# Gate products of w_down queued on VectorE behind the step they are written in; the samples' rows of w_down loaded in the other order

## The chip, the cores and the metric

The kernel runs on one core of one Trainium2 chip. The metric is the device time of one execution in microseconds (us), the median of several. A core has five engines, each with an instruction queue of its own that is worked off in order: PE (TensorE, matrix products; PEld is its weight load), DVE (VectorE), ACT (ScalarE), POOL (GpSimd) and SP (SyncE, which here only issues DMAs). Times in rows of the trace count from the first instruction of the profiled execution.

## The reference

One layer of a hybrid recurrent decoder: a token mixer with three head groups, then a gated feed-forward part, for a prompt of 2048 tokens and 8 sample sequences of 4 tokens, all in fp32. The change lies in the feed-forward part:

```python
h = _rmsnorm(x, p['norm_ffn'][l]) * (1 + sc2) + sh2
gate, b_ffn = _causal_dwconv(h @ p['ffn_w_gate'][l], b_ffn, p['ffn_conv_w'][l])
gate = gate + p['ffn_conv_b'][l]
x = x + g2 * ((jax.nn.silu(gate) * (h @ p['ffn_w_up'][l])) @ p['ffn_w_down'][l])
```

The model width is 1024 and the feed-forward width 2816. `g2` is a vector of 1024 numbers per sequence, so for the prompt it can be multiplied into the columns of `ffn_w_down` ahead of the product.

## The kernel before

The program is written in Python as a sequence of steps. A scheduler then orders the instructions of each engine by a simulation of its own: an instruction may be queued ahead of others that are written earlier, where its data allow it and the simulated engine is free. So the place where an instruction is written does not fix its place in its engine's queue. The function that adds an edge "not ahead of this instruction, on the same engine, without a semaphore" is `issue_after`.

Every fp32 product is made of three passes: an operand is split into a rounded part (`w_hi`, a cast on ACT, L1815) and a rest (`w_lo`, a subtraction on DVE, L1816), and PE multiplies hi by hi (L1824), hi by lo and lo by hi (L1825, L1826).

The second half of the prompt goes through a Strassen scheme. In its up stage (`ffn_up_s`), the weights of gate and up come as sets of four 512-column pieces (`w_raw`, 9 buffers). POOL forms sums of these pieces (L1797 to L1803, `s_combo`), ACT and DVE split them into one of four buffers of `w_hi` and `w_lo`, and PE runs seven products a set, each for two groups of tokens, 12 matmuls a product and group, into banks `s_x`, `s_y`, `s_v`. Behind a product (`after`), ACT takes a copy of a bank (`sn`, L1985), DVE adds banks and copies (`add`, L2031) or multiplies up by gate (`mul`, L2032), and the convolution and the activation run on DVE (L1999, L2011, L665), ACT and POOL. PE may write on into a bank only when these readers are done. The sequence has 32 plain products and 140 Strassen products.

Beside this, `down_sums` prepares the weights of the later down stage. It has 11 rows. For each it loads four pieces of `ffn_w_down` (`t_raw`, 8 buffers, so two rows), multiplies each by the gate `g` on DVE (L2176: the gate products, 44 in all), forms four differences on POOL (L2183, 44) and stores the eight results into `wdT` in DRAM (88 stores on SP). The program writes one piece of a row behind each step, from step 40 on, so that 11 rows are written over some 99 of the 172 steps. Nothing of the up stage reads these results: the down stage (`ffn_down_s`) loads them again, from `wdT` into `t_raw`.

In the down stage, `samples` multiplies the 32 sample tokens by the 22 row blocks of the plain `ffn_w_down`: two loads of 128 by 512 for each (`h` 0 and 1, the two halves of the columns), then four small matmuls (L2240, `mm_ds`) that read the half 0, 0, 1, 1.

Of the kernel before, what the change touches and what calls it, by code (L numbers as in the profile page):

```python
# [14 lines left out]
ALU = mybir.AluOpType  # L15
# [59 lines left out]
class Kern:  # L75
# [1840 lines left out]
    def ffn_up_s(self, pts, open1, down):  # L1916

        nc = self.nc
# [64 lines left out]
        def snap(c, ps):  # L1983
            t = self.pev.tile([128, NP], F32, name="sn", tag="sn", bufs=SSN)
            nc.scalar.copy(t, ps)  # L1985
            return t
# [3 lines left out]
        def conv(f, g, U):  # L1990

            n, ns = GS[g][1:]
            y = self.pev.tile([128, NW2], F32, name="sy", tag="ey", bufs=SEY)
            N = n + ns
            cw = self.fcw
            nc.gpsimd.tensor_copy(U[:, 0:2], self.fhalo[:, f, :])
            nc.scalar.activation(y, U[:, 2:], AF.Identity, scale=cw[:, 2, f:f + 1], bias=self.fcb[:, f:f + 1])
            for k in (1, 0):
                nc.vector.scalar_tensor_tensor(y[:, :n], U[:, k:k + n], cw[:, k, f:f + 1], y[:, :n],  # L1999
                                               op0=ALU.mult, op1=ALU.add)  # L2000
            if g == 0:
                nc.gpsimd.tensor_copy(self.fhalo[:, f, :], U[:, n:n + 2])
            else:
                nc.gpsimd.tensor_copy(self.ftails[:, f, 0:2], U[:, n:n + 2])
            if ns:
                us = self.pev.tile([128, NSEQ, NTOK + 2], F32, name="cv_s", tag="cv_s", bufs=2)
                nc.gpsimd.tensor_copy(us[:, :, 0:2], self.sffn[:, f, :].rearrange("p (s k) -> p s k", k=2))
                nc.gpsimd.tensor_copy(us[:, :, 2:], U[:, 2 + n:2 + N].rearrange("p (s t) -> p s t", t=NTOK))
                ys = y[:, n:N].rearrange("p (s t) -> p s t", t=NTOK)
                for k in (1, 0):  # L2010
                    nc.vector.scalar_tensor_tensor(ys, us[:, :, k:k + NTOK], cw[:, k, f:f + 1], ys,  # L2011
                                                   op0=ALU.mult, op1=ALU.add)
                nc.gpsimd.tensor_copy(self.ftails[:, f, 2:18].rearrange("p (s k) -> p s k", k=2), us[:, :, NTOK:])
            hold[f, g] = y

            def act():
                self.silu(y, U[:, 2:], y)
            self.later(1, act)

        def put(f, g, y):  # L2020
            t0 = GS[g][0]
            self.st(self.dram["aT"][f * 128:(f + 1) * 128, t0:t0 + NW2], y)

        def gate_u():
            return self.pev.tile([128, 2 + NW2], F32, name="su", tag="cu", bufs=4)

        def after(s, g, P):
            kind, j, _ = sets[s]
            c = ctx[s, g]
            f1, f2 = 2 * j, 2 * j + 1  # L2030
            add = lambda o, a, b: nc.vector.tensor_tensor(o, a, b, op=ALU.add)  # L2031
            mul = lambda o, b: nc.vector.tensor_tensor(o, o, b, op=ALU.mult)  # L2032
            if P[0] == "C":
                f, h = (f1, f2)[int(P[1]) - 1], (lo_, hi_)[int(P[2]) - 1]
                ps = c[PLAIN_BANK[P]]
                if kind == "u":
                    mul(hold[f, g][:, h], ps)
                    if P[2] == "2":
                        put(f, g, hold.pop((f, g)))
                    return  # L2040
                if P[2] == "1":
                    c[f] = gate_u()
                nc.scalar.copy(c[f][:, 2 + h.start:2 + h.stop], ps)
                if P[2] == "2":
                    conv(f, g, c[f])
                return
            if P in "12":
                if P == "1":
                    c["s1"] = snap(c, c["X"])
                c["n"] = c.get("n", 0) + 1  # L2050
                if c["n"] < 2:
                    return
                s1 = c["s1"]
                if kind == "g":
                    c["U1"] = gate_u()
                    add(c["U1"][:, 2:2 + NP], c["Y"], s1)
                else:
                    add(s1, c["Y"], s1)
                    mul(hold[f1, g][:, lo_], s1)
            elif P == "5":  # L2060
                c["s5"] = snap(c, c["V"])
            elif P == "6":
                c["s2"] = snap(c, c["X"])
            elif P == "3":
                if kind == "g":
                    add(c["U1"][:, 2 + NP:], c["V"], c["s2"])
                    conv(f1, g, c["U1"])
                else:
                    add(c["s2"], c["V"], c["s2"])
                    mul(hold[f1, g][:, hi_], c["s2"])  # L2070
                    put(f1, g, hold.pop((f1, g)))
            elif P == "7":
                if kind == "g":
                    c["U2"] = gate_u()
                    add(c["U2"][:, 2 + NP:], c["X"], c["s5"])
                else:
                    add(c["s5"], c["X"], c["s5"])
                    mul(hold[f2, g][:, hi_], c["s5"])
            elif P == "4":
                if kind == "g":  # L2080
                    nc.scalar.copy(c["U2"][:, 2:2 + NP], c["X"])
                    conv(f2, g, c["U2"])
                else:
                    mul(hold[f2, g][:, lo_], c["X"])
                    put(f2, g, hold.pop((f2, g)))
# [67 lines left out]
    def down_sums(self):  # L2153


        nc = self.nc
        w = self.i["ffn_w_down"][0].rearrange("(k p) c -> p k c", p=128)
        g = self.pev.tile([128, D], F32, name="g2", tag="g2", bufs=1)
        self.ld(g, self.ap(self.dram["modr"], 5 * D, [[0, 128], [1, D]]))
        row = 0  # L2160
        for n, kh in enumerate(KH):
            k0 = 2 * sum(KH[:n])
            for k in range(kh):
                q = {}
                for x in ("11", "12", "22", "21"):
                    i, j = int(x[0]) - 1, int(x[1]) - 1
                    q[x] = r = self.w_raw()[:, :512]
                    self.ld(r, w[:, k0 + kh * i + k, 512 * j:512 * j + 512])

                def put(P, x):  # L2170
                    self.st(self.dram["wdT"]["123B567".index(P) if P != "4" else 7, row], q[x])
                for _ in range(2):
                    yield
                for x, P in (("11", "1"), ("12", "B"), ("22", "3"), ("21", "2")):
                    j = int(x[1]) - 1
                    nc.vector.tensor_tensor(q[x], q[x], g[:, 512 * j:512 * j + 512], op=ALU.mult)  # L2176
                    put(P, x)
                    if x in ("12", "21"):
                        yield
                yield  # L2180
                for P, o, a, b in (("5", "11", "12", "11"), ("7", "12", "22", "12"), ("6", "22", "22", "11"),
                                   ("4", "21", "21", "22")):
                    nc.gpsimd.tensor_tensor(q[o], q[a], q[b], op=ALU.subtract)  # L2183
                    yield
                    put(P, o)
                row += 1
# [37 lines left out]
    def ffn_down_s(self, p, pts, work, freed):  # L2224


        nc = self.nc
# [8 lines left out]
        def sample(k, raw):  # L2236

            done.append(k)
            for j in range(4):
                nc.tensor.matmul(pss[32 * j:32 * j + 32, :256], sam[:, k, :],  # L2240
                                 raw[j // 2][:, 256 * (j % 2):256 * (j % 2) + 256],
                                 start=(len(done) == 1), stop=(len(done) == NFB), tile_position=(0, 32 * j))

        def samples():
            w = self.i["ffn_w_down"][0].rearrange("(k p) c -> p k c", p=128)
            r = []
            for k in range(NFB + 1):
                if k < NFB:
                    r.append([self.w_raw()[:, :512] for _ in range(2)])
                    for h in range(2):  # L2250
                        self.ld(r[k][h], w[:, k, 512 * h:512 * h + 512])
                    yield
                if k:
                    sample(k - 1, r[k - 1])
# [129 lines left out]
        for m, (s, P, U, t, b, begins, ends) in enumerate(seq):  # L2384
            n, q = sets[s]
# [348 lines left out]
```

## Time and profile before

| what | value |
|---|---|
| runs | 2830.92, 2831.51, 2834.84 us, median 2831.51 |
| the profiled execution's own time | 2829.4 us |
| its span, first to last instruction | 2827.7 us |
| mean granted TensorE clock | 0.984 |
| the Strassen up stage on PE (`s_x`, first to last matmul) | 1833.5 to 2339.7 us |
| first and last start of a gate product (L2176) | 1888.2 and 2046.9 us |
| sample products (`mm_ds`) on PE | 2358.2 to 2537.2 us |

A page has a row for each engine with the busy time and the share of the span, and then the span in 40 slices, a digit each: the busy share in tenths, for PEclk the granted clock in tenths of full speed. A row of groups names line, engine, operation and tiles, then the count, the busy time, the mean length of one in ns, and the idle time of the engine ahead of them with what ended it. A row of windows gives, for a stretch, its length and for each engine the busy time with the instruction count behind it, then granted clock, DMA share and GB/s. PE is 96% busy over the whole span, so a time that PE loses in one stretch is not hidden by anything else.

### The profile page before, as it was taken

The numbers are of one execution on the slowest core, as the hardware profiler recorded it, in microseconds if no ns is written. First come the engines' busy times: TensorE is split into PE (matmuls) and PEld (weight loads), VectorE is DVE, ScalarE is ACT, GpSimd is POOL, SyncE is SP. The second block draws the span as 40 slices with busy tenths as digits, with TensorE's granted clock in tenths as the row PEclk, the third lists the DMA queues.
The fourth block names the chain that finished last, engine by engine and source line by source line (L and its number), as shares of the span: only waits on it lengthen the run. The fifth ranks groups of instructions, "written<-read, shape, count | busy, mean of one in ns | idle before, by whom it ended". The sixth has DMA issues, their size and how long they took to land.

```text
span 2827.7 us, 54627 instructions
## 1 busy us (share of the span) xinstructions
PE 2709.6 (96%) x19969; PEld 2461.6 (87%) x19969; DVE 1848.7 (65%) x3785; ACT 1235.5 (44%) x2732; POOL 804.9 (28%) x1272
## 2 busy tenths in 40 slices
PE   6999999999999999999999999988899999999998
PEld 4999888889889999999999989978799996678786
DVE  4535677576666778665565546599976775465765
ACT  4544545455554545544434323443344452232433
POOL 3311223211112422121211101258853441213232
PEclk8999999999999999999999999999999999999999
DMA  6465436575646697554543444687732239786652
GB/s 235 139 203 153 127 111 176 179 228 137 183 151 207 211 288 197 164 150 129 174 143 108 118 144 145 194 255 265 266 120 84 86 91 308 220 285 195 220 167 97
DMA packets 566867, 498.58 MB, mean 176 GB/s; under 512 B 85942, under 2 KB 477782, under 8 KB 565574
## 3 DMA queue, kind: packets, MB, share of 16 engines
q1 hardware_dynamic: 566598, 495.09, 56.8%
q8 instruction: 157, 2.57, 0.4%
q14 instruction: 112, 0.92, 0.1%
HBM read 330.36 MB, written 164.60 MB: 175 GB/s over the span
## 4 chain that ended last, share of the span: by engine, by line
PE 73%; DMA 10%; DVE 8%; issue 3%; ACT 3%; POOL 2%; SPq 1%; DVEq 0%; POOLq 0%; ACTq 0%
PE mm_f L610 10%; PE mm_f L612 10%; PE mm_f L611 10%; PE d_ps L1824 5%; PE d_ps L1826 5%; PE d_ps L1825 5%; PE s_x L1824 2%; PE s_x L1825 2%; PE s_x L1826 2%; PE mm_t L653 2%; PE mm_t L654 1%; PE mm_t L656 1%; DMA w_raw<-oT 1%; DVE w_lo L1816 1%; PE ssq L729 1%
## 5 line engine op out<-in xcount | busy, mean ns | idle before, releaser
L610 PE MATMUL mm_f<-g_hi,w_hi 128*128 128x384 f32 (+2 forms) x2016 | 662.4, 329 | 4.5 <-ACT g_hi L581 4.5
L611 PE MATMUL mm_f<-g_lo,w_hi 128*128 128x384 f32 (+2 forms) x2016 | 652.4, 324 | 0.4 <-DVE g_lo L582 0.4
L612 PE MATMUL mm_f<-g_hi,w_lo 128*128 128x384 f32 (+2 forms) x2016 | 652.0, 323 | 0.0
L610 PEld LDWEIGHTS mm_f<-g_hi,w_hi 128*128 128x128 f32 x2016 | 381.5, 189 | 25.9 <-issue 14.6
L611 PEld LDWEIGHTS mm_f<-g_lo,w_hi 128*128 128x128 f32 x2016 | 382.2, 190 | 6.7 <-issue 4.8
L612 PEld LDWEIGHTS mm_f<-g_hi,w_lo 128*128 128x128 f32 x2016 | 381.8, 189 | 6.4 <-issue 5.7
L1824 PE MATMUL d_ps<-t_hi,w_hi 128*128 128x512 f32 x627 | 250.0, 400 | 5.6 <-ACT w_hi L1815 3.6
L1825 PE MATMUL d_ps<-t_lo,w_hi 128*128 128x512 f32 x627 | 247.3, 395 | 0.0
L1826 PE MATMUL d_ps<-t_hi,w_lo 128*128 128x512 f32 x627 | 243.5, 398 | 0.6 <-DVE w_lo L1816 0.6
L1824 PE MATMUL s_x<-t_hi,w_hi 128*128 128x264 f32 x704 | 204.1, 290 | 20.1 <-ACT sn L1985 8.6
L1826 PE MATMUL s_x<-t_hi,w_lo 128*128 128x264 f32 x704 | 201.7, 288 | 11.3 <-DVE w_lo L1816 11.2
L558 DVE TENSOR_TENSOR w_lo<-w_raw,w_hi 128x512 fp32r<-128x512 f32 (+1 forms) x236 | 163.9, 701 | 73.8 <-ACT w_hi L557 70.3
L1815 ACT CAST w_hi<-a_raw 128x512 fp32r<-128x512 f32 (+1 forms) x159 | 92.8, 584 | 266.2 <-PE d_ps L1825 200.2
L557 ACT CAST w_hi<-w_raw 128x512 fp32r<-128x512 f32 (+1 forms) x236 | 144.2, 619 | 138.6 <-PE mm_f L611 97.0
L1825 PE MATMUL s_x<-t_lo,w_hi 128*128 128x264 f32 x704 | 202.2, 287 | 0.0
L2334 DVE TENSOR_TENSOR d_y<-d_ps,d_y 128x512 f32<-128x512 f32 x159 | 108.8, 687 | 139.0 <-PE d_ps L1826 134.0
L1816 DVE TENSOR_TENSOR w_lo<-w_raw,w_hi 128x512 fp32r<-128x512 f32 x156 | 126.5, 813 | 56.0 <-ACT w_hi L1815 55.3
L1815 ACT CAST w_hi<-w_raw 128x512 fp32r<-128x512 f32 x156 | 96.3, 619 | 147.4 <-PE s_x L1825 50.4
L1824 PEld LDWEIGHTS d_ps<-t_hi,w_hi 128*128 128x128 f32 x627 | 118.1, 188 | 45.3 <-ACT w_hi L1815 11.0
L1824 PEld LDWEIGHTS s_x<-t_hi,w_hi 128*128 128x128 f32 x704 | 134.5, 191 | 23.5 <-ACT sn L1985 9.8
L683 DVE SCALAR_TENSOR_TENSOR qy<-cv_u,par,qy 128x384 f32<-128x384 f32 (+1 forms) x216 | 122.8, 571 | 38.9 <-POOL cv_u L674 23.5
L1826 PEld LDWEIGHTS d_ps<-t_hi,w_lo 128*128 128x128 f32 x627 | 118.1, 188 | 31.6 <-DVE d_y L2334 2.9
(572 smaller groups left out, 6671.3 us busy)
## 6 DMA issues: line engine op xcount, KB each, us to landing
w_raw<-in_w_in_dram SPq DMA_DIRECT2D x96, 256.0 KB
d_y<-x SPq DMA_DIRECT2D x96, 256.0 KB
w_raw<-in_ffn_w_gate_dram SPq DMA_DIRECT2D x94, 256.0 KB
w_raw<-in_ffn_w_up_dram SPq DMA_DIRECT2D x94, 256.0 KB
t_raw<-in_ffn_w_down_dram SPq DMA_DIRECT2D x88, 256.0 KB
wdT<-t_raw SPq DMA_DIRECT2D x88, 256.0 KB
t_raw<-wdT SPq DMA_DIRECT2D x88, 256.0 KB
ada_w<-in_w_ada_dram SPq DMA_DIRECT2D x32, 512.0 KB
```

The lines of the kernel that those rows point to most:

```text
L557: nc.scalar.copy(hi[:, :n], raw[:, :n])
L558: nc.vector.tensor_sub(lo[:, :n], raw[:, :n], hi[:, :n].bitcast(F32))
L610: nc.tensor.matmul(ps[:, :N], wh, hi[:, k, :N], start=(k == 0), stop=False)
L611: nc.tensor.matmul(ps[:, :N], wh, lo[:, k, :N], start=False, stop=False)
L612: nc.tensor.matmul(ps[:, :N], wl, hi[:, k, :N], start=False, stop=(k == 7))
L683: nc.vector.scalar_tensor_tensor(y[:, :n], u[:, j:j + n], cw[:, j, blk:blk + 1], y[:, :n], op0=ALU.mult, op1=ALU.add)
L1815: self.nc.scalar.copy(hi, src)
L1816: self.nc.vector.tensor_sub(lo, src, hi.bitcast(F32))
L1824: self.nc.tensor.matmul(ps, hi[:, k], th, start=(start and k == 0), **f)
L1825: self.nc.tensor.matmul(ps, hi[:, k], tl, start=False, **f)
L1826: self.nc.tensor.matmul(ps, lo[:, k], th, start=False, stop=(k == n - 1), skip_group_check=True)
L2334: add = lambda name, ps: nc.vector.tensor_tensor(xs[s, name], ps, xs[s, name], op=ALU.add)
```

## The change

Two edits. The first remembers the last `add` or `mul` of the up stage that was written (`self.pace`) and writes each gate product inside `issue_after`, so that DVE has it no earlier than behind that instruction. The second swaps the order in which the two halves of a samples' row are loaded. The number of instructions on every engine, their shapes and their data stay the same.

```diff
-            add = lambda o, a, b: nc.vector.tensor_tensor(o, a, b, op=ALU.add)
-            mul = lambda o, b: nc.vector.tensor_tensor(o, o, b, op=ALU.mult)
+            def add(o, a, b):
+                self.pace = nc.vector.tensor_tensor(o, a, b, op=ALU.add)
+
+            def mul(o, b):
+                self.pace = nc.vector.tensor_tensor(o, o, b, op=ALU.mult)
...
                 for x, P in (("11", "1"), ("12", "B"), ("22", "3"), ("21", "2")):
                     j = int(x[1]) - 1
-                    nc.vector.tensor_tensor(q[x], q[x], g[:, 512 * j:512 * j + 512], op=ALU.mult)
+                    with self.tc.issue_after(self.pace.ins):
+                        nc.vector.tensor_tensor(q[x], q[x], g[:, 512 * j:512 * j + 512], op=ALU.mult)
                     put(P, x)
...
-                    for h in range(2):
+                    for h in (1, 0):
                         self.ld(r[k][h], w[:, k, 512 * h:512 * h + 512])
```

Three places show what the scheduler makes of it. A row is a line of the program, the operation, the tiles written and read, the shape, and a count where equal instructions follow each other. The gate product's line is L2176 before and L2180 now; L2031, L2032 and L2183 become L2032, L2035 and L2187.

DVE's queue where the last plain sets end and the first gate product stood, before:

```order
L1811 TENSOR_TENSOR t_raw<-t_raw 128x528
L2176 TENSOR_TENSOR t_raw<-t_raw,g_23409 128x512
L1816 TENSOR_TENSOR w_lo<-w_raw,w_hi 128x512
L1816 TENSOR_TENSOR t_lo<-t_raw,t_hi 128x528 x2
L2032 TENSOR_TENSOR sy<-sy,s_y 128x264 x2
L2176 TENSOR_TENSOR t_raw<-t_raw,g_23409 128x512
L1816 TENSOR_TENSOR w_lo<-w_raw,w_hi 128x512
L665 SCALAR_TENSOR_TENSOR sy<-su,sy 128x528
L1816 TENSOR_TENSOR t_lo<-t_raw,t_hi 128x528
L2176 TENSOR_TENSOR t_raw<-t_raw,g_23409 128x512 x2
L1816 TENSOR_TENSOR t_lo<-t_raw,t_hi 128x528
```

The same place now:

```order
L1811 TENSOR_TENSOR t_raw<-t_raw 128x528
L1816 TENSOR_TENSOR w_lo<-w_raw,w_hi 128x512
L1816 TENSOR_TENSOR t_lo<-t_raw,t_hi 128x528 x2
L2035 TENSOR_TENSOR sy<-sy,s_y 128x264 x2
L1816 TENSOR_TENSOR w_lo<-w_raw,w_hi 128x512
L665 SCALAR_TENSOR_TENSOR sy<-su,sy 128x528
L1816 TENSOR_TENSOR t_lo<-t_raw,t_hi 128x528 x2
```

The gate products are gone from here. Counted over DVE's whole queue by the splits of weights (rows `w_lo<-w_raw`, one for each piece of weights that PE is fed, 156 in the up stage), the first gate product stands behind the 30th split where it stood behind the 17th, and the last behind the 120th where it stood behind the 59th: 44 products over 90 splits in place of 42.

DVE's queue now at the second of the eleven rows of `w_down`, where its four products stand together:

```order
L2011 SCALAR_TENSOR_TENSOR sy<-cv_s,par_970,sy 128x32
L2032 TENSOR_TENSOR su<-s_x,sn 128x264
L2180 TENSOR_TENSOR t_raw<-t_raw,g_23409 128x512 x4
L665 SCALAR_TENSOR_TENSOR sy<-su,sy 128x528
L1999 SCALAR_TENSOR_TENSOR sy<-su,par_970,sy 128x496
L2011 SCALAR_TENSOR_TENSOR sy<-cv_s,par_970,sy 128x32
L1816 TENSOR_TENSOR w_lo<-w_raw,w_hi 128x512
```

They stand behind an add that frees a bank, and ahead of the next split of a weight. Of the eleven rows, six have their four products split into two pairs at two places, and the other five have them in a lump of four like this one.

POOL's queue, where the differences of `down_sums` stand among the sums of weights (L1797 to L1803), in the third Strassen set before:

```order
L1799 TENSOR_TENSOR w_raw<-w_raw 128x512
L2007 COPY cv_s<-sffn 128x8x2
L1801 TENSOR_TENSOR w_raw<-w_raw 128x512
L2183 TENSOR_TENSOR t_raw<-t_raw 128x512 x6
L2007 COPY cv_s<-sffn 128x8x2
L2183 TENSOR_TENSOR t_raw<-t_raw 128x512 x2
L1797 TENSOR_TENSOR w_raw<-w_raw 128x512
```

And the first differences now:

```order
L1797 TENSOR_TENSOR w_raw<-w_raw 128x512
L2187 TENSOR_TENSOR t_raw<-t_raw 128x512
L1803 TENSOR_TENSOR w_raw<-w_raw 128x512
L2187 TENSOR_TENSOR t_raw<-t_raw 128x512 x2
L1799 TENSOR_TENSOR w_raw<-w_raw 128x512
L2187 TENSOR_TENSOR t_raw<-t_raw 128x512
L1801 TENSOR_TENSOR w_raw<-w_raw 128x512
```

Eight differences stood in a row ahead of a sum; now one or two stand between sums here, and at most four anywhere. SP's stores into `wdT` and the loads of `ffn_w_down` move along: the last store stands 12 loads of weights, three sets, ahead of the end of the up stage's 96 loads, where it stood 46 loads ahead.

## The prediction, made before the changed kernel ran

> **What bounds the kernel now.** I read the page first, for the engine that is busy and the slices in which it isn't.
>
> ```profile
> span 2827.7 us, 54627 instructions
> PE 2709.6 (96%) x19969; PEld 2461.6 (87%) x19969; DVE 1848.7 (65%) x3785; ACT 1235.5 (44%) x2732; POOL 804.9 (28%) x1272
> ...
> PE   6999999999999999999999999988899999999998
> ...
> DVE  4535677576666778665565546599976775465765
> ...
> POOL 3311223211112422121211101258853441213232
> ```
>
> PE is busy for 96% of the span. Only the first slice, the last, and slices 27 to 29 (70.7 us each, from 1838 us) fall below nine tenths, and in these three DVE and POOL stand at their highest. So I asked for windows around them, with the bounds at the first gate product and the end of the last.
>
> ```profile
> 1860.00:1888.00 28.00, 21.40 (x163) 20.13 (x163) 27.78 (x35) 15.60 (x29) 19.62 (x18) 1.00 0.63 195
> 1888.00:2048.00 160.00, 131.04 (x981) 127.33 (x982) 157.55 (x196) 53.65 (x109) 130.73 (x106) 0.94 0.79 264
> 2048.00:2100.00 52.00, 50.50 (x414) 50.07 (x413) 39.22 (x66) 21.66 (x43) 28.50 (x31) 1.00 0.50 159
> 2100.00:2300.00 200.00, 200.00 (x1649) 200.00 (x1649) 140.09 (x247) 91.25 (x177) 86.02 (x111) 1.00 0.25 75
> 2358.00:2540.00 182.00, 178.24 (x805) 121.71 (x804) 96.61 (x158) 50.22 (x93) 35.82 (x32) 1.00 0.83 273
> ```
>
> The columns behind the length are busy time and count of PE, PEld, DVE, ACT and POOL, then the granted clock, the DMA share and GB/s. From 2100 to 2300 us the same matmuls run with nothing in the way: 1649 / 200 = 8.245 a microsecond. Against that pace 1888 to 2048 holds 981 / 8.245 = 119.0 us of work in 160 us, a **loss of 41.0 us**. (PE's idle time there, 29.0 us, says less, as the granted clock is 0.94.) From 2048 to 2100 it is 52 - 414 / 8.245 = 1.8 us, and from 1860 to 1888, ahead of all gate products, 28 - 163 / 8.245 = 8.2 us. DVE is busy for 98.5% of the 160 us and for 70% of the undisturbed stretch. The waits of PE from 1888 to 2060 us say who ended them:
>
> ```profile
> PE s_x L1826 <- DVE w_lo L1816: 10.5, 3, 5.3
> PE s_x L1824 <- ACT sn L1985: 8.6, 6, 3.5
> PE s_x L1824 <- DVE sy L2032: 4.7, 1, 4.7
> PE s_x L1824 <- DVE sn L2031: 4.3, 4, 1.6
> ```
>
> DVE ends most of them. ACT was held up in its turn by POOL, as the timeline around 1995 us shows:
>
> ```profile
> 1999.41 0.62 ACT L1815 CAST w_hi<-w_raw 128x512 fp32r<-128x512 f32 x1 [7.00 <-POOL w_raw L1797]
> ...
> 1994.72 2.97 POOL L2183 TENSOR_TENSOR t_raw<-t_raw 128x512 f32<-128x512 f32 x2
> 1997.65 1.73 POOL L1797 TENSOR_TENSOR w_raw<-w_raw 128x512 f32<-128x512 f32 x1
> ```
>
> Two differences of `down_sums` stood ahead of the sum that ACT needed, and ACT idled for 7.00 us with the copies of banks queued behind.
>
> **What the gate products cost where they stand.** The groups of DVE and POOL from 1888 to 2048 us (first five rows), and of DVE from 2100 to 2300 (last three):
>
> ```profile
> L2176 DVE TENSOR_TENSOR t_raw<-t_raw,g 128x512 f32<-128x512 f32 x44 | 44.7, 1026 | 0.5 <-DMA t_raw<-in_ffn_w_down_dram 0.5
> L1816 DVE TENSOR_TENSOR w_lo<-w_raw,w_hi 128x512 fp32r<-128x512 f32 x42 | 42.0, 1008 | 0.1
> L2032 DVE TENSOR_TENSOR sy<-sy,sn 128x264 f32<-128x264 f32 x14 | 13.4, 972 | 0.0
> L1816 DVE TENSOR_TENSOR t_lo<-t_raw,t_hi 128x528 fp32r<-128x528 f32 x4 | 4.9, 1236 | 0.0
> L2183 POOL TENSOR_TENSOR t_raw<-t_raw 128x512 f32<-128x512 f32 x41 | 65.4, 1596 | 11.9 <-DVE t_raw L2176 4.4 <-DVE su L2031 2.6 <-DMA wdT<-t_raw 2.3
> ...
> L1816 DVE TENSOR_TENSOR w_lo<-w_raw,w_hi 128x512 fp32r<-128x512 f32 x69 | 50.8, 736 | 37.6 <-ACT w_hi L1815 37.0
> L2032 DVE TENSOR_TENSOR sy<-sy,sn 128x264 f32<-128x264 f32 x30 | 17.6, 588 | 0.7
> L665 DVE SCALAR_TENSOR_TENSOR sy<-su,sy 128x528 f32<-128x528 f32 x20 | 14.0, 699 | 1.0 <-ACT su L664 1.0
> ```
>
> All 44 gate products fall into the 160 us. They take 44.7 us themselves, and everything else on DVE that reads two tiles is longer while POOL works: the split of a weight 1008 ns against 736, the product into `sy` 972 against 588. In sum, DVE's load that goes with PE's progress is 0.70 x 119.0 = 83.4 us, and 5.6 us belong to the last splits of tokens (`t_lo` 4.9, and one sum of 0.7). What is left of 157.55 is 68.6 us, or **1.56 us for a gate product with its difference on POOL**. So DVE was asked for 157.6 us of work in the 119.0 us that PE needed: it was the bound there, and PE followed it.
>
> **The change, part by part.** The first edit spreads the same 44 products, with their 44 differences on POOL and 88 stores on SP, over 90 splits of weights in place of 42. A split comes every 200 / 69 = 2.90 us at PE's full pace, so that is 261 us, from some 13 splits (38 us) later than 1888 on. DVE's load in them is 0.70 x 261 = 182.8, plus 68.6, together 251.4 us or **96% of 261**. In the 160 us DVE kept itself 98.5% busy, so its floor is 251.4 / 0.985 = 255 us, just under what PE needs. PE becomes the bound again, and of the loss of 41.0 + 1.8 = 42.8 us only what the two engines cost each other at so small a margin stays.
>
> That rest is not in the trace of before as such. Its lower end is 0, as from 2100 to 2300 us. For the upper end I take the two windows with the fewest gate products among others, ten in 40 us:
>
> ```profile
> 1940.00:1960.00 20.00, 18.39 (x151) 18.18 (x150) 20.00 (x27) 5.87 (x12) 17.41 (x11) 1.00 0.85 280
> 1960.00:1980.00 20.00, 18.41 (x148) 17.78 (x146) 18.72 (x26) 7.70 (x13) 16.68 (x21) 1.00 0.82 265
> ```
>
> They hold 299 / 8.245 = 36.3 us of work in 40, a loss of 10%, which would be 26 us over 261. Their density is 0.25 products a microsecond, the changed kernel's 44 / 261 = 0.17. A loss that grows in proportion would give 17 us, one that grows with the square 11 to 12. I take 11, as waiting grows faster than load, and keep 0 and 26.
>
> Every instruction of a moved row was looked at. On SP, 88 stores and 44 loads move from a stretch with 264 GB/s into one with 75 GB/s, which hides them; their buffers hold two rows, so a row's loads are issued a row, some 24 us, ahead of its products. On POOL, 86.02 / 200 = 43% of 261 us and 44 x 1.6 us make 70% where it was 82%, and fewer differences stand ahead of a sum. The late end is covered too: behind the last gate product 36 splits, 36 x 2.90 = 104 us, are still to come ahead of the first use of `wdT`. The loss of 8.2 us from 1860 to 1888 stays, being older than the first gate product.
>
> The second edit I cost at nothing. PE's four small products of a row read both halves anyway. PE idles for 182 - 178.24 = 3.8 us in the stretch that holds them, which is all there is to gain; a second half that comes one issue later could cost 22 times that issue, 22 x 0.383 = 8.4 us, if nothing covered it:
>
> ```profile
> L133 SPq DMA_DIRECT2D t_raw<-in_ffn_w_down_dram x88: 327/383/1389, 1882.1 to 2512.5; - x88
> ```
>
> (In this row the three numbers are minimum, median and maximum in ns.) The eight buffers let loads run up to four rows ahead, so 0 is the value near to both.
>
> The sum is 42.8 - 11 = 31.8 us less. Against the profiled execution's own 2829.4 us that gives 2797.6; the median of the runs shown stands 2.1 us above that execution, and I say **2798 us**. With 26 and with 0 left it is 2812 and 2787.
>
> **The rivals.** *DVE stays the bound.* The 1.56 us are an average in which the two engines partly missed each other. If each difference on POOL held up DVE for its whole length, a product would cost 0.68 us (the shortest) and 1.58 to 1.60 us, together 44 x 2.27 = 100 us. DVE would need (182.8 + 100) / 0.985 = 287 us, 26 more than PE, and with the same 11 us of friction the gain shrinks to 6 to 17 us: 2812 to 2824, say 2818. For it speaks how a gate product's length spreads:
>
> ```profile
> L2176 DVE TENSOR_TENSOR t_raw<-t_raw,g x44: 674/680/1798, 1888.2 to 2046.9; 128x512 f32<-128x512 f32 x44
> ```
>
> The longest is 1.12 us above the median, most of a difference's 1.6 us; against it speaks that half of them show no delay at all. The Trainium skill, "SBUF — State Buffer", section "Who interferes with whom", states this as a rule: a DVE instruction with two SBUF inputs and a GpSimd instruction that reads SBUF exclude each other, the later one blocking fully until the first has ended. By that rule moving products gains DVE no time, and the sum would come out at this rival's 2818; the measured 68.6 us lie under the rule's 100, since DVE isn't hurt while it is idle or reads a bank.
>
> *Nothing changes.* The stall could hang on POOL's queue (the 7.00 us above) more than on DVE. Then up to four differences ahead of a sum, 4 x 1.6 = 6.4 us, would stop ACT once a row as eight did before. At 3.9 us a row, 11 rows eat the 42.8 us: about 2829.
>
> *Slower.* The lumps of four take DVE 4 x 0.68 = 2.7 us at best and 4 x 1.80 = 7.2 us at worst, with the next split queued behind, and the pairs half of that. Four buffers of `w_lo` give the split a lead of at most three products, 3 x 2.90 = 8.7 us. If a lag of DVE from the step before uses up that lead, each lump reaches PE whole, and each pair by half: 5 x 7.2 + 12 x 3.6 = 79 us, against 42.8 saved, 2866. It decides from 3.9 us a row on. At little over that it is 2840.
>
> **How the numbers follow.** The forecast, 2787 to 2812, has a chance of 0.70; DVE as the bound 0.15; nothing 0.07; slower 0.08. All but the last two are faster by over 0.2% (5.7 us, about what a measurement of this kernel can tell from no change): faster 0.85, same 0.07, slower 0.08. The range takes the forecast's own and most of the first rival, 2786 to 2820.
>
> **What would show it.** In the changed kernel gate products should start near 1925 us and end near 2190; the window 1888 to 2048 should hold some 1250 to 1320 matmuls where it held 981; DVE should be busy for 90 to 97% between the first and the last of them; the last matmul into `s_x` should come near 2308 us instead of 2339.7. The split of a weight should shrink from 1008 ns to 800 to 900; at 1000 and more the first rival has it. PE waiting for `w_lo` behind lumps of four would show the slower case, ACT waiting for L1797 to L1803 the unchanged one. A shift of more than 5 us in 2358 to 2540 would prove the cost of the second edit wrong.

## The result and the profile after

The changed kernel takes **2809.53 us** (2805.47 to 2814.03, four runs) where the kernel before took 2831.22 us on the same chip: a ratio of 0.9921, 95% interval 0.9903 to 0.9940. It is faster by 21.7 us; the prediction said 2798 us, 32 us faster, with a range of 2786 to 2820. The profiled execution took 2811.16 us. Its page:

```profile
span 2809.1 us, 54626 instructions
PE 2706.4 (96%) x19969; PEld 2461.8 (88%) x19969; DVE 1844.4 (66%) x3785; ACT 1236.4 (44%) x2732; POOL 805.4 (29%) x1272
...
PE   6999999999999998999999999989999999999998
...
DVE  4535777677676777665665556588798875475765
...
POOL 3311223211112422121122101246566541213232
```

Of the three weak slices of PE (27 to 29) two are back at nine tenths; the third, from 1826 us, holds the loss that lies ahead of the gate products. DVE's three 9s in a row have become 8 8 7 9 8 8 7. The windows of the changed kernel, with the columns as before (length, then busy time and count of PE, PEld, DVE, ACT and POOL, granted clock, DMA share, GB/s):

```profile
1860.00:1888.00 28.00, 21.73 (x170) 20.68 (x168) 26.78 (x32) 15.40 (x29) 19.16 (x19) 0.99 0.66 205
1888.00:2048.00 160.00, 152.87 (x1206) 151.53 (x1207) 131.41 (x204) 65.37 (x129) 100.60 (x102) 0.96 0.51 168
2048.00:2100.00 52.00, 50.40 (x401) 49.99 (x400) 47.90 (x73) 25.64 (x52) 33.54 (x33) 0.97 0.55 178
2100.00:2200.00 100.00, 97.29 (x780) 96.29 (x779) 89.87 (x128) 37.66 (x75) 69.56 (x64) 0.98 0.57 192
2200.00:2300.00 100.00, 96.95 (x783) 96.36 (x782) 72.78 (x120) 44.20 (x86) 46.48 (x58) 0.98 0.36 114
```

From 1888 to 2048 us there are 1206 matmuls where there were 981. At the full pace of 8.245 matmuls a microsecond the last four rows lose 13.7, 3.4, 5.4 and 5.0 us, 27.5 together where the kernel before lost 42.8. So a good part of the loss is not gone but spread, into stretches that had none. (Of the 13.7 us, 4.1 lie from 1888 to 1900 us, ahead of the first gate product; that row stands in the last section.) Where the gate products, the splits of weights and the Strassen stage lie now (count; minimum, median and maximum in ns; first and last start):

```profile
L2180 DVE TENSOR_TENSOR t_raw<-t_raw,g x44: 673/680/1791, 1922.3 to 2205.3; 128x512 f32<-128x512 f32 x44
...
L1816 DVE TENSOR_TENSOR w_lo<-w_raw,w_hi x156: 673/684/1795, 1830.8 to 2315.9; 128x512 fp32r<-128x512 f32 x156
...
L1824 PE MATMUL s_x<-t_hi,w_hi x704: 280/284/587, 1834.5 to 2325.0; 128*128 128x264 f32 x176
```

The up stage, from the first to the last of these matmuls, takes 490.5 us where it took 506.2 (1833.5 to 2339.7). It is the same work in every kernel below but for what is left out beside it, so its length serves as a measure. The rest of the span, behind it, went from 2827.7 - 2339.7 = 488.0 to 484.1 us. What PE, and then ACT for its casts, waited for in the changed kernel (us in total, times, longest; PE from 1888 to 2330 us, ACT from 1920 to 2220):

```profile
PE s_v L1824 <- ACT w_hi L1815: 4.9, 2, 2.6
PE s_x L1824 <- ACT sn L1985: 4.6, 2, 2.9
PE s_x L1826 <- DVE w_lo L1816: 4.1, 4, 1.6
...
ACT w_hi L1815 <- POOL w_raw L1799: 41.1, 12, 6.3
ACT w_hi L1815 <- POOL w_raw L1801: 14.4, 11, 2.3
ACT w_hi L1815 <- POOL w_raw L1797: 13.7, 4, 4.1
```

Before, DVE ended most of PE's waits; now ACT ends more than half, and ACT waits for POOL's sums of weights for 69.2 us (49.0 before, in the same window). The groups of DVE and POOL from 1920 to 2220 us (count, busy us, mean ns, idle time ahead and what ended it):

```profile
L1816 DVE TENSOR_TENSOR w_lo<-w_raw,w_hi 128x512 fp32r<-128x512 f32 x96 | 86.6, 905 | 26.3 <-ACT w_hi L1815 25.8
L2180 DVE TENSOR_TENSOR t_raw<-t_raw,g 128x512 f32<-128x512 f32 x44 | 34.8, 839 | 0.0
...
L2187 POOL TENSOR_TENSOR t_raw<-t_raw 128x512 f32<-128x512 f32 x44 | 71.0, 1614 | 43.5 <-DMA wdT<-t_raw 19.3 <-DVE sy L1999 9.1 <-DVE t_raw L2180 8.6
```

Three suspects can be read from this. POOL's differences stand in its queue ahead of the sums, for 71.0 us of their own and 43.5 us of waiting, 19.3 of it for stores of the tiles that they overwrite. DVE's splits take 905 ns in the mean, where the median of the stage is 684 and the shortest 673. And DVE has its products in lumps. The waits alone suggested the queue; the experiments put more of the loss on the slowing.

### The profile page after: what moved, and what is told of

Its sections match the earlier page's. It is cut to its first block, busy times and chain, and to the rows that moved or that the text cites. A ratio compares the mean times of both kernels' runs of the same rounds, so it can differ in the third digit from the quotient of the medians.

```text
span 2809.1 us, 54626 instructions
## 1 busy us (share of the span) xinstructions
PE 2706.4 (96%) x19969; PEld 2461.8 (88%) x19969; DVE 1844.4 (66%) x3785; ACT 1236.4 (44%) x2732; POOL 805.4 (29%) x1272
## 4 chain that ended last, share of the span: by engine, by line
PE 57%; DMA 8%; DVE 7%; issue 3%; POOL 2%; ACT 2%; SPq 1%; DVEq 0%; POOLq 0%; ACTq 0%
PE mm_f L610 8%; PE mm_f L612 7%; PE mm_f L611 7%; PE d_ps L1824 5%; PE d_ps L1826 5%; PE d_ps L1825 4%; PE s_x L1824 2%; PE s_x L1826 2%; PE s_x L1825 2%; DMA rb<-rows 2%; DVE w_lo L1816 1%; DMA w_raw<-oT 1%; PE s_y L1824 1%; PE s_y L1825 1%; PE s_y L1826 1%
## 5 line engine op out<-in xcount | busy, mean ns | idle before, releaser
L610 PEld LDWEIGHTS mm_f<-g_hi,w_hi 128*128 128x128 f32 x2016 | 380.5, 189 | 26.5 <-issue 14.6
L653 PE MATMUL mm_t<-w_hi,g_hi 128*128 128x260 f32 (+1 forms) x544 | 141.0, 294 | 5.3 <-ACT g_hi L2467 4.4
```

The costliest lines, as they stand in the source:

```text
L610: nc.tensor.matmul(ps[:, :N], wh, hi[:, k, :N], start=(k == 0), stop=False)
L653: nc.tensor.matmul(ps[:m, :nc_], a, wh[:, k % 2], start=(k == 0), stop=False)
```

## The experiments

Each run is compared with the kernel before on its own chip (there 2822 to 2824 us in the median), so ratios are what to compare: the changed kernel's is 0.9921, from the first chip; it was not run again beside them. Profiled executions can lie several microseconds off the median of their kernel, so where a ratio and the length of a stage differ, the ratio decides.

**Each edit alone.** The first kernel keeps the old order of loads, the second keeps the old gate products:

```diff
-                    for h in (1, 0):
+                    for h in range(2):
                         self.ld(r[k][h], w[:, k, 512 * h:512 * h + 512])
```

> The first edit alone (gate products behind the step they are written in), the samples' rows loaded in the old order. If the second edit costs and brings nothing, as predicted, this runs as the changed kernel does: 2806 to 2813 us, and the stretch behind the last product into s_x takes the 484 us that it takes in the changed kernel. If the 4 us by which that stretch is shorter in the changed kernel (484 against 488 us) come from the order of the samples' loads, it takes 488 us here and the time is 2812 to 2817 us.

> The second edit alone: the kernel before with the samples' rows loaded in the other order. If it costs and brings nothing: 2831 us, within 2 us, with the stretch behind the last product into s_x at 488 us. If it is what shortens that stretch: 2826 to 2828 us and 484 us.

The first edit alone gives 0.9938 (0.9922 to 0.9954), the second alone 0.9989 (0.9980 to 0.9998). The stretch behind the up stage is 488.1 us with the first alone (2804.2 - 2316.1) and 486.9 us with the second alone (2821.9 - 2335.0), beside 488.0 before and 484.1 with both. So the first edit brings some 17.5 us, and the second about 3 us of its own (0.6 to 5.6 by its interval), near the 3.8 us that PE idled in that stretch and not quite the nothing that it was put at. The gain lies in the sample products, first the kernel with the first edit alone, then the changed kernel:

```profile
L2244 PE MATMUL mm_ds<-t_raw,d_sam x176: 378/379/404, 2334.6 to 2516.1; 128*32 128x256 f32 x176
...
L2244 PE MATMUL mm_ds<-t_raw,d_sam x176: 379/379/404, 2343.4 to 2521.0; 128*32 128x256 f32 x176
```

From the first to the last of them it is 181.5 and 177.6 us, beside 179.2 before and 178.1 with the second edit alone.

**Half of the pair left out.** Without the differences, and without the products (the differences then held behind the last sum written, `self.sum`, so that they keep their place):

```diff
-                    nc.gpsimd.tensor_tensor(q[o], q[a], q[b], op=ALU.subtract)
```

> The changed kernel without the 44 differences on POOL in down_sums (the tiles are stored undifferenced, so this part of w_down's sums is left out); products, loads and stores stay where they are. The changed kernel loses 27.5 us against PE's full pace from 1888 to 2300 us. Theory A (the differences stand in POOL's queue ahead of the weights' sums, ACT waits behind these, and PE behind ACT): 20 to 27 of them go, 2783 to 2790 us, the windows run at 8.2 matmuls a microsecond, and ACT's waits for L1797 to L1803 of over 1 us are gone. Theory B (DVE's load of 96%, with the lumps of products, is what PE waits for): DVE's load falls only by the part that the differences lock, PE goes on waiting for w_lo behind the lumps, and 10 us or more stay: 2793 us or more.

```diff
...
-                    with self.tc.issue_after(self.pace.ins):
-                        nc.vector.tensor_tensor(q[x], q[x], g[:, 512 * j:512 * j + 512], op=ALU.mult)
...
-                    nc.gpsimd.tensor_tensor(q[o], q[a], q[b], op=ALU.subtract)
+                    with self.tc.issue_after(self.sum.ins):
+                        nc.gpsimd.tensor_tensor(q[o], q[a], q[b], op=ALU.subtract)
```

> The changed kernel without the 44 gate products on DVE (the gate's factor in w_down is left out); the differences stay on POOL, each held behind the last sum of weights written before it, so that they keep their place (8th to 64th sum) without the products that they hung on. Theory A (POOL's queue): the stalls through ACT stay, two thirds of the loss of 27.5 us, 2798 to 2806 us. Theory B (DVE's load): DVE loses 30 us of work and its lumps, PE waits no more, 2783 to 2790 us.

Without differences the ratio is 0.9858 (0.9845 to 0.9871), without products 0.9875 (0.9863 to 0.9888). In ratios, theory A had stood at 0.983 to 0.9855 and at 0.988 to 0.991 for the two, theory B at 0.9865 or more and at 0.983 to 0.9855. Each result lies between the two: either half can go, and most of what was left goes with it. The kernel without differences (`w_lo` from 1920 to 2220 us, and the up stage), then the one without products:

```profile
L1816 DVE TENSOR_TENSOR w_lo<-w_raw,w_hi 128x512 fp32r<-128x512 f32 x104 | 80.1, 771 | 44.8 <-ACT w_hi L1815 43.1 <-DMA w_raw<-in_ffn_w_gate_dram 1.1
...
L1824 PE MATMUL s_x<-t_hi,w_hi x704: 279/284/422, 1831.8 to 2296.7; 128*128 128x264 f32 x176
```

```profile
L1815 DVE TENSOR_TENSOR w_lo<-w_raw,w_hi 128x512 fp32r<-128x512 f32 x100 | 90.1, 903 | 42.0 <-ACT w_hi L1814 39.0 <-DMA t_raw<-in_ffn_w_down_dram 2.2
...
L1823 PE MATMUL s_x<-t_hi,w_hi x704: 281/284/422, 1829.9 to 2303.8; 128*128 128x264 f32 x176
```

The up stage takes 464.9 us without differences; 506.2 - 42.8 = 463.4 is what the prediction had for no loss at all. So the changed kernel's rest is 490.5 - 464.9 = **25.6 us**. Without products the splits are as slow as ever (903 ns), and still only 473.9 - 464.9 = 9.0 us of it are left: slow splits by themselves cost PE no more than that, and cost more with the products beside them. (POOL's waits ahead of the differences went with the products, from 43.5 to 1.1 us, so this kernel does not part the slowing from those waits.)

**Other places for the differences.** Held behind the last sum; the same and three steps later, beside the next row; one directly behind a sum each, handed over by `down_sums`; and on DVE:

```diff
...
-                    nc.gpsimd.tensor_tensor(q[o], q[a], q[b], op=ALU.subtract)
+                    with self.tc.issue_after(self.sum.ins):
+                        nc.gpsimd.tensor_tensor(q[o], q[a], q[b], op=ALU.subtract)
```

> The changed kernel with each difference on POOL held behind the last sum of weights written before it; still up to four differences in a row between two sums. In the changed kernel (ratio 0.992) POOL idles for 43.5 us just ahead of its 44 differences: 19.3 us for stores of the tiles that they overwrite, 8.6 us for the products, the rest for DVE. Theory C (these waits, not the differences' own time, hold up the sums behind them, and ACT and PE behind the sums): the differences come a little later, POOL's idle time ahead of them falls somewhat, 0.989 to 0.992. Theory D (DVE, slowed by POOL's differences and given the products in lumps, is what PE waits for): no change, 0.991 to 0.993.

```diff
...
+            for _ in range(1 + 3):
+                yield
             for P, o, a, b in (("5", "11", "12", "11"), ("7", "12", "22", "12"), ("6", "22", "22", "11"),
...
```

> As the one with pinned differences, and each row's differences come three steps later (beside the next row's loads), so that the stores of the products have landed; products and the distance of rows stay. Theory C: POOL's idle time ahead of the differences falls from 43.5 to under 10 us, and with it half or more of the 18 us that the changed kernel loses beyond the two kernels with one part left out: 0.986 to 0.989. Theory D: the same DVE work and the same slowing, 0.991 to 0.993.

```diff
...
+            if P in "5637" and self.due:
+                with self.tc.issue_after(self.sum.ins):
+                    nc.gpsimd.tensor_tensor(*self.due.pop(), op=ALU.subtract)
...
```

> The differences spread singly: one directly behind a sum of weights on POOL, so that at most one stands ahead of any sum, and none before its row's products are stored; rows may get a few steps longer. Theory C: no wait ahead of a difference and at most 1.6 us ahead of a sum, 0.985 to 0.988. Theory D: DVE's products stay in their lumps and the slowing stays, 0.990 to 0.993. If it is under 0.9921 by more than the interval it beats both kernels.

```diff
-                    nc.gpsimd.tensor_tensor(q[o], q[a], q[b], op=ALU.subtract)
+                    with self.tc.issue_after(self.pace.ins):
+                        nc.vector.tensor_tensor(q[o], q[a], q[b], op=ALU.subtract)
```

> The changed kernel with the 44 differences on DVE, behind the step they are written in, in place of POOL. POOL's queue is free of them, and DVE is no longer slowed by them: its load goes from 251 to about 183 + 88 x 0.68 = 243 us of the 261. Theory C: the sums come early and ACT's waits for them go, but DVE itself now waits for the stores; 0.988 to 0.991. Theory D by DVE's load and lumps alone: 93% instead of 96%, PE goes on waiting for w_lo, 0.991 to 0.994. Theory D by the slowing alone (two engines on two-input instructions): the slowing is gone, 0.986 to 0.988.

Pinned: 0.9908 (0.9896 to 0.9921). Later: 0.9896 (0.9882 to 0.9911). One behind a sum: 0.9921 (0.9906 to 0.9935). On DVE: **0.9870** (0.9856 to 0.9883). Pinned, the result lies in theory C's range and a hair under theory D's. The differences three steps later, on POOL from 1880 to 2220 us:

```profile
L2185 POOL TENSOR_TENSOR t_raw<-t_raw 128x512 f32<-128x512 f32 x44 | 69.4, 1578 | 8.0 <-DMA wdT<-t_raw 6.0 <-issue 1.3
```

The waits ahead of the differences fell from 43.5 to 8.0 us, as theory C asked, but the ratio only from 0.9921 to 0.9896, with intervals that overlap: between the 0.986 to 0.989 of C and the 0.991 to 0.993 of D. Spreading them singly brought nothing, as D had it: with at most one ahead of a sum, ACT waited for sums even longer, 90.6 us (68.2 + 17.0 + 5.4). Moving them to DVE, which gives the busy engine more to do, brought the most, as D had it for the slowing alone, and its interval lies wholly below the changed kernel's (0.9903 to 0.9940). That kernel from 1920 to 2220 us, the window and then two groups:

```profile
1920.00:2220.00 300.00, 298.57 (x2450) 297.74 (x2449) 265.01 (x455) 131.30 (x261) 160.95 (x157) 1.00 0.59 194
...
L1816 DVE TENSOR_TENSOR w_lo<-w_raw,w_hi 128x512 fp32r<-128x512 f32 x102 | 77.3, 760 | 23.0 <-ACT w_hi L1815 22.9
L2188 DVE TENSOR_TENSOR t_raw<-t_raw 128x512 f32<-128x512 f32 x44 | 37.2, 845 | 2.0 <-DMA wdT<-t_raw 1.8
```

And the changed kernel in the same window:

```profile
1920.00:2220.00 300.00, 290.05 (x2316) 287.69 (x2316) 257.81 (x382) 120.22 (x240) 195.39 (x191) 0.98 0.56 186
```

With the differences on DVE it is busier, 265.0 us of 300 against 257.8, and PE loses 300 - 2450 / 8.245 = 2.8 us against 300 - 2316 / 8.245 = 19.1. So the share of DVE's time that is taken is not what PE's loss follows. (For each matmul DVE has a little less to do, 108 ns against 111; the kernel with a tile more, below, leaves that out as a reason.) The splits' length fits: 760 ns against 905. A difference took 1614 ns on POOL and takes 845 on DVE.

**The slowing and the queue taken apart.** This run keeps POOL's queue full but takes away its reads: each difference becomes a fill of the same tile, which waits for the same stores.

```diff
-                    nc.gpsimd.tensor_tensor(q[o], q[a], q[b], op=ALU.subtract)
+                    nc.gpsimd.memset(q[o].bitcast(mybir.dt.uint8)[:, :1792], 0)
```

> The changed kernel with each of the 44 differences on POOL replaced by a fill of 128 x 1792 bytes of the same tile with zeros (the differences are left out; by the fills of this trace, 2.03 us for 128 x 2304 elements, one should take about 1.6 us). POOL's queue is as full as in the changed kernel and the fill waits for the same stores, but it reads nothing from SBUF. Theory D (POOL's differences slow DVE's instructions, whose end PE waits for): DVE's split of a weight falls from 905 to about 770 ns, as in the kernel without differences, and the ratio to 0.986 to 0.989. Theory F (their time and waits in POOL's queue delay the sums): split times fall or not, the ratio stays 0.990 to 0.993.

The ratio is 0.9878 (0.9856 to 0.9900), below the changed kernel's interval by a hair. On its chip the changed kernel with a tile more (below; ratio 0.9927) took 2801.38 to 2810.72 us, this one 2786.28 to 2794.95. DVE's split and POOL's fill, ACT's waits for the sums, and the up stage:

```profile
L1816 DVE TENSOR_TENSOR w_lo<-w_raw,w_hi 128x512 fp32r<-128x512 f32 x99 | 74.8, 762 | 41.1 <-ACT w_hi L1815 40.4
L2187 POOL MEMSET t_raw<- 128x1792 uint8 x44 | 69.0, 1590 | 48.2 <-DMA wdT<-t_raw 48.2
...
ACT w_hi L1815 <- POOL w_raw L1799: 40.7, 14, 6.5
ACT w_hi L1815 <- POOL w_raw L1797: 17.3, 5, 4.2
ACT w_hi L1815 <- POOL w_raw L1801: 11.6, 11, 2.1
...
L1824 PE MATMUL s_x<-t_hi,w_hi x704: 279/284/422, 1831.5 to 2307.4; 128*128 128x264 f32 x176
```

POOL's queue is as full as in the changed kernel (69.0 us against 71.0), stands still ahead of the fills even longer (48.2 against 43.5), and ACT waits for sums as long as there (69.6 us against 69.2). Yet more than half of the gain that leaving out the differences brings is there, 0.0043 of 0.0063 by the ratios and 14.6 of 25.6 us by the stages, and the split takes 762 ns. Theory D has it: the larger part of what PE lost comes from POOL's differences slowing DVE's instructions. Whether the rest is the queue's stays open. The Trainium skill, "SBUF — State Buffer", section "Who interferes with whom", states that a DVE instruction with two SBUF inputs contends with a GpSimd instruction that reads SBUF and not with one that only writes it; this pair of traces agrees, 905 against 762 ns.

**The loop of sums.** One more tile for product 6's sum, paid for with one of the seven buffers of `sn`, in the changed kernel and in the one with the differences on DVE:

```diff
-SRAW, SW, SWR, SEY, SSN = 9, 4, 8, 6, 7
+SRAW, SW, SWR, SEY, SSN = 10, 4, 8, 6, 6
...
-            t(q["s"], q["s"], q["11"], op=ALU.subtract)
+            old, q["s"] = q["s"], new()
+            t(q["s"], old, q["11"], op=ALU.subtract)
```

> The changed kernel with one more tile for the sums of weights: product 6's sum goes into a tile of its own (ten buffers for nine, six for the snapshots of banks in place of seven) and no longer waits until DVE has split product 5's sum in the same tile. Theory E (sum, cast, split and the next sum in place are one loop through POOL, ACT and DVE of about 1.5 + 0.6 + 0.75 = 2.9 us, as long as PE's step of 2.9 us, so that any difference or gate product in it makes PE late): 0.986 to 0.990, and POOL's waits for w_lo shrink. Without it: 0.991 to 0.994, or worse by the missing snapshot buffer.

> The kernel with the differences on DVE (0.987) and the tile of its own for product 6's sum. Theory E: another 2 to 8 us, 0.984 to 0.986. If the loop doesn't matter once POOL is free of the differences: 0.986 to 0.988.

The changed kernel with it: 0.9927 (0.9905 to 0.9949), so nothing. ACT's wait for a sum in it (the only row of that kind from 1920 to 2220 us), and PE's largest in total (1888 to 2290 us):

```profile
ACT w_hi L1816 <- POOL w_raw L1800: 2.9, 1, 2.9
...
PE s_x L1825 <- DVE sn L2033: 9.0, 6, 2.9
```

ACT's waits for the sums are all but gone, 2.9 us where there were 69.2, and the time did not move, against theory E: PE waits for DVE instead. (It has one buffer of `sn` less, which may have cost what was gained.) With the differences on DVE the extra tile gives **0.9853** (0.9830 to 0.9875), the lowest ratio of all and below the changed kernel's interval, so this kernel is faster than the one before and the changed one. The number lies where theory E had it, but against 0.9870 without the tile it can't be told apart. Its window:

```profile
1920.00:2220.00 300.00, 299.34 (x2457) 298.57 (x2456) 273.52 (x454) 132.18 (x258) 149.88 (x157) 1.00 0.60 196
```

DVE has as much to do for each matmul as in the changed kernel (273.52 / 2457 and 257.81 / 2316 are both 111 ns) and is busier in the 300 us, yet PE loses 300 - 2457 / 8.245 = 2.0 us. So DVE's load alone does not explain the 19.1.

**Wider spacing.** Eleven steps to a row in place of nine:

```diff
                 row += 1
+                yield
+                yield
```

> The changed kernel with eleven steps to a row of w_down in place of nine, so that the 44 products and differences lie over 11/9 of the stretch. The stage up to the last product into s_x takes 490.5 us in the changed kernel and 464.9 without the differences: 25.6 us that the pairs of product and difference cost. If each pair costs the same wherever it stands (a cost in proportion to their number), spreading wins nothing more: 488 to 492 us, ratio 0.991 to 0.993. If the cost grows with the square of their density, as the prediction had it, 25.6 x 9/11 = 21 us stay: 486 us, ratio 0.990 to 0.991. If they then come late for w_down, the stretch behind the last product into s_x is longer than 484 us.

0.9913 (0.9900 to 0.9927): on the side of a small gain, but within the interval of 0.9921. The up stage takes 2304.0 - 1822.8 = 481.2 us, under the 486 and the 488 to 492 of both laws, but this profiled execution is 7.2 us faster than the median of its kernel. So it does not decide between the two laws. The stretch behind the up stage is 2786.9 - 2304.0 = 482.9 us, so the rows did not come late.

In one table (stage: first to last matmul into `s_x`, by the one profiled execution; split and waits from 1920 to 2220 us):

| kernel | ratio | stage, us | split, ns | ACT waiting for sums, us |
|---|---|---|---|---|
| the changed kernel | 0.9921 | 490.5 | 905 | 69.2 |
| own tile for a sum | 0.9927 | 488.3 | 908 | 2.9 |
| one difference behind a sum | 0.9921 | 486.0 | 891 | 90.6 |
| eleven steps to a row | 0.9913 | 481.2 | 826 | 62.2 |
| differences pinned | 0.9908 | 486.4 | 913 | 71.7 |
| differences later | 0.9896 | 486.4 | 864 | 69.9 |
| fills in place of differences | 0.9878 | 475.9 | 762 | 69.6 |
| no products | 0.9875 | 473.9 | 903 | 60.3 |
| differences on DVE | 0.9870 | 468.7 | 760 | 57.7 |
| no differences | 0.9858 | 464.9 | 771 | 41.1 |
| on DVE, own tile | 0.9853 | 469.6 | 732 | none |

Among kernels that keep the products, those with splits of 732 to 771 ns have ratios of 0.9853 to 0.9878 and those with 826 to 913 ns have 0.9896 to 0.9927; within each group there is no clear order. (With eleven steps only 34 of the 44 products lie in that window.) ACT's waits for sums show no such split, though they are the largest numbers in the views. The kernel without products stands apart: slow splits, but little lost.

## Why the prediction was right in kind and short in size

- **DVE was the bound, and spreading its load frees PE: right.** The first products start at 1922 us (forecast 1925), the last at 2205 (2190). With nothing in the way the up stage would gain 42.8 us; the kernel without differences, which leaves their collisions out as well, has 506.2 - 464.9 = 41.3. The kernel before was not run with its differences on DVE or as fills, so how much of its loss was DVE's load and how much the collisions is argued from its rows, not shown.
- **DVE's load: near.** The step had 1.56 us for a product with its difference and 96% of the stretch. From 1920 to 2220 us DVE was busy for 257.81 us, and PE did 2316 / 8.245 = 280.9 us of work; less 0.70 x 280.9 = 196.6 that leaves 61.2 us or 1.39 us a pair, and 86% of the 300 us, not 90 to 97%.
- **"The rest that stays": the step that failed.** It was put at 11 us, between bounds of 0 and 26, with the reason that waiting grows faster than load. It measured 25.6 us against the kernel without differences (27.1 against the 463.4 of no loss), at the upper bound. In proportion to the density, from the same two windows of before, it would have been 17. The premise was wrong too: the rest does not follow how full DVE is (with the differences on DVE it is fuller and PE loses 2.8 us in 300, with the own tile 2.0), but comes in the larger part from single DVE instructions that POOL's reads stretch, up to 1.79 us for a product of 0.68, where products and splits stand together. Spreading the products leaves as many differences to meet DVE's splits, 905 ns where 800 to 900 was forecast. Of the 25.6 us the profile of the kernel with fills gives 490.5 - 475.9 = 14.6 to the slowing and 11.0 to POOL's queue. By the ratios the slowing is 0.9921 - 0.9878, some 12 us, and the queue's part can't be told from nothing, as 0.9878 and 0.9858 have intervals that overlap. How large the queue's part is stays open.
- **The second edit at nothing: off by some 3 us**, inside its bounds (3.8 us to gain). The shift of over 5 us that would have refuted it did not come: the sample products take 177.6 us where they took 179.2.
- **The sum**, by the profiled executions: the up stage takes 490.5 us where 506.2 - 31.8 = 474.4 was forecast, 16.1 more; it starts 1.0 us later (1834.5 against 1833.5) and 3.9 us are gained behind it. 2797.6 + 16.1 + 1.0 - 3.9 = 2810.8, and 2811.16 was measured. The 1206 matmuls (1250 to 1320 forecast) and the last matmul into `s_x` at 2325.0 us (2308) are the same miss. That the time still lies under the 2812 us of the forecast's own upper end is luck in part: the first edit alone, at 0.9938, would be at some 2814.
- **The rivals.** "DVE stays the bound" had the right cause, POOL's differences holding up DVE, but the wrong price: 1.39 us a pair and not 2.27, and DVE is not full. "Nothing changes" hung on POOL's queue; its sign came, ACT waiting for L1797 to L1803 for 69.2 us, but two kernels, one with as much of that wait and one with almost none, show that the time hardly follows it. For "slower", the lumps of four would have had to reach PE with 3.9 us a row; PE's longest wait for `w_lo` is 1.6 us.

## What to carry to other kernels

Two elementwise engines that run side by side can each have idle time and still cost the third: compare an instruction's mean length in the crowded stretch with its minimum, and if it is stretched, try the work on the engine that is stretched before spreading it thinner. Here 44 subtractions on the busier DVE cost less (845 ns each) than on the idler POOL (1614 ns, and a split 145 ns longer in the mean). And a long wait in a view is a suspect, not a price: take it away once and see whether the time follows.

## What the hardware showed that was not expected

Stalls of PE cost more than their length here, as the granted clock is lower right behind them. In the changed kernel, behind the losses from 1860 to 1888 us (clock 0.99):

```profile
1888.00:1900.00 12.00, 10.52 (x65) 10.00 (x66) 11.96 (x18) 4.24 (x8) 8.47 (x5) 0.74 0.60 188
```

PE was busy for 10.52 of 12 us but got through 65 matmuls where 99 fit, at a clock of 0.74: of the 4.1 us that it lost only 1.5 are idle time. Its matmuls from 1890.4 to 1894.1 us took 0.42 us each, against a median of 284 ns. This lies ahead of the first gate product and is in the kernel without differences too (clock 0.50 from 1884 to 1888 us), so no gate product caused it.
